# A transformer-like layer on one core: operand builders ordered behind the bank copies, their splits two products behind their loads, and the sums of the FFN down weights made in FFN up

## The chip, the core and the metric

The kernel runs on one core of one Trainium2 chip. The metric is the time of one execution on the device in microseconds (us). Before the change three executions took 1679.03, 1671.73 and 1673.55 us, median 1673.55. The core has a matrix engine (TensorE, PE in the profile, with its weight loads as PEld), two elementwise engines that matter here (VectorE = DVE, ScalarE = ACT), GpSimd (POOL) and the sync engine (SP), which issues nearly all DMAs. The program lists the instructions of each engine in one order, and the trace shows each elementwise engine and SP go through its list in that order; engines wait for each other through semaphores.

## The reference, cut to what matters

One layer over 1024 positions of width 1024, all in float32:

- `h = RMSNorm(x)`, then one wide product `h @ w_in` (1024 to 7168 columns) whose parts feed a retention branch (4 heads, chunked recurrence, group norm, swish gate) and a gated linear recurrence (causal convolution, block-diagonal gates, a scan over positions, GeLU gate).
- Each branch has an output product (`w_ret_o`, `w_lru_o`, 1024 x 1024), the two are merged by sigmoid gates, and `x = x + mix @ w_out`.
- `h = RMSNorm(x)`; `gate, val = split(h @ ffn_w_up)` (1024 to 2 x 3072); a causal convolution of width 3 and GeLU on `gate`; `x = x + (gelu(gate) * val) @ ffn_w_down` (3072 to 1024). A last RMSNorm gives the output.

## The kernel before, in words

**How a product is made exact enough.** Every float32 operand tile of 128 x 512 is split into two reduced-precision float32 tiles: `split` (L165) casts on ScalarE (`hi`, L168) and subtracts on VectorE (`lo`, L169). One product then takes three matmul passes (`PASSES`, L111): hi*hi, hi*lo, lo*hi. An operand tile costs one ScalarE and one VectorE instruction and holds two tile buffers.

**Jobs.** A job computes 256 x 1024 outputs from a 256 x 1024 block of weights (the stationary side, `A11..A22`) and an operand kept on chip (`op`, keys `B11, B12, B21, B22` with j = 0..3, each a split pair). A standard job (`mm_std`, L317; matmuls on L331) takes 8 products of 12 matmuls. A fast job (`mm_fast`, L378; matmuls on L388) is a Strassen-like scheme with 7 products of 12 matmuls; it needs the sums `T1 = B12 - B11`, `T2 = B22 - T1`, `T3 = B12 - B22`, `T4 = B21 - T2` of the operand, split too. In the fast job the bank X is used in a chain: after a product `keep` (L400) copies X on ScalarE (L403), and only then may the next product of X accumulate onto it. `total` (L412) adds a bank to a copy on VectorE (L414), `more` (L406) adds an earlier result read from DRAM (L409). The order of the products is A11 B11, S1 T1, S2 T2, A12 B21, S3 T3, A22 T4, S4 B22, and the first product of the next job is put ahead of the last of the present one.

**Two streams beside the products.** At the end of each product the program calls `build(BRATE)` (L286) and `advance(RATE)` (L304). `build` steps generators in `builders`, which make the operand of a later stage: `operand` (L984) loads 16 blocks and splits them, up to 3 loads ahead of the one it splits (`reads`, L532), then `tsets` (L540) loads the same 16 blocks again, makes the four sums for one j after another (subtractions on L545, L548, L551, L553) and splits them. A step has a cost, and a call of `build` spends up to 3.0: five splits at 0.6. It stops while fewer than 20 of the 81 buffers (`NU`, 128 x 512 float32 each) are free (`RESERVE`). `need` (L296) forces the builder when a product asks for a key that isn't there. `advance` steps the generators in `back`, the work that follows a job (recurrence, retention, and the like), by one unit.

**What sets the order.** The instructions are traced in program order with priorities (`NOW` 3000 for the bank copies and adds, `SOON` 400 for the builders), and a scheduler then lists them engine by engine, once, before the run. It takes the instruction of highest priority among those which its own model of times holds ready. So an instruction of a builder may be listed ahead of a bank copy which is traced earlier, when the model has its data there first. On the chip the engine then waits in that order.

**Where builders work.** `og` (operand of the four standard ret_o jobs, from DRAM tensor `og_d`) is built during the last job of the input product; `u` (from `u_d`, for lru_o: one standard and three fast jobs) during the last ret_o job and the standard lru_o job; `h2` (for FFN up, from tiles on chip) at the start of FFN up; and `dop[0..2]`, the FFN down weights `w_dn` in three groups g, each used by one standard and three fast jobs (t = 0..3). `dop[0]` is built from the last FFN up job on, `dop[g+1]` from job t = 3 of group g on. FFN down adds up its three groups in DRAM (`x1_d`): from_x1 (L1262) reads, L1276 writes. FFN up is 24 jobs, whose `post_ff` (L1208) writes `ff_d`, which FFN down reads as its stationary side.

In the profile's names buffer numbers and digits are left out: `u` is one of the 81 buffers, `w` one of 22 weight buffers, `g` and `a` are PSUM banks, `x_d` is `x1_d` and `t_d` is `t1_d`.

Of the kernel before, what the change touches and what calls it, by code (L numbers as in the profile page):

```python
# [11 lines left out]
F32 = mybir.dt.float32  # L12
# [5 lines left out]
P = 128  # L18
D = 1024
T = 1024  # L20
KT = 8
TH = 512
# [64 lines left out]
class Units:  # L87
# [11 lines left out]
    def get(self, dt=F32):  # L99
        i = self.q.popleft()  # L100
        self.count += 1
        t = self.pool.tile(self.shape, dt, tag=f"{self.name}{i}", name=f"{self.name}{i}_{self.count}")
        self.at[id(t)] = (i, t)
        return t
# [3 lines left out]
            self.q.append(self.at.pop(id(t))[0])  # L108


PASSES = ((0, 0), (0, 1), (1, 0))  # L111
NU = 81
NW = 22
# [3 lines left out]
RATE = 1.0  # L117
BRATE = 3.0
RESERVE = 20
NOW, SOON, OLD = 3000, 400, 800  # L120
FAST_RO = 0
RO_T = 9
# [7 lines left out]
def tile_trunk_layer(ctx, tc, x, xt, positions, params, consts, normf, w_in, w_ro, w_lo,  # L130
# [23 lines left out]
    sg_d = pdr.tile([2, KT, P, T], F32, tag="sg", name="sg_d")  # L154
    t1_d = pdr.tile([KT, P, T], F32, tag="t1", name="t1_d")
    x1_d = pdr.tile([T, D], F32, tag="x1", name="x1_d")
    ff_d = pdr.tile([3, 8, 2, P, 4, P], F32, tag="ff", name="ff_d")

    def pc(name, i):
# [2 lines left out]
    def hp(offset=1500):  # L162
        return tc.high_priority(offset=offset)

    def split(src, get=get):  # L165

        hi, lo = get(F32R), get(F32R)
        S.copy(hi, src)  # L168
        V.tensor_sub(lo, src, hi.bitcast(F32))  # L169
        return hi, lo  # L170

    def drop(s):
        put(*s)
# [4 lines left out]
    class Job:  # L178
        def __init__(self, src, op, emit, post=None, fast=False, last=False, drop12=False,
                     pre=None, fetch=None, order=None):  # L180
            self.pre = pre
            self.order = order or (("A11", "A21", "A22", "A12") if fast else ORD_T)
            self.fetch, self.got = fetch, {}
            self.src, self.op, self.emit, self.post = src, op, emit, post
            self.fast, self.last, self.drop12 = fast, last, drop12
            self.raw, self.blk = {}, {}
# [8 lines left out]
            return self.got.pop((m, h))  # L195

    queue = []
    state = {"load": None, "prep": None, "blocks": 0, "raws": 0, "hp": False}

    def loads():  # L200
        i = 0
# [83 lines left out]

    def build(budget, reserve=RESERVE):  # L286

        with hp(SOON):
            while builders and budget > 0 and len(U) >= reserve:
                c = next(builders[0], None)  # L290
                if c is None:
                    builders.popleft()
                else:
                    budget -= c

    def need(op, key):  # L296
        with hp(SOON):
            while key not in op:
                if next(builders[0], None) is None:
                    builders.popleft()  # L300
        return op[key]


# [74 lines left out]
    def mm_fast(jb, op):  # L378
        X, Y, Z = psg.get(), psg.get(), psg.get()

        def prod(bank, an, bn, first):
            pump((jb, an))
            w = jb.blk[an]
            n = 0
            for j in range(4):
                c = slice(128 * j, 128 * j + 128)
                for a, b in PASSES:
                    PE.matmul(bank, w[a][:, c], need(op, (bn, j))[b], start=first and n == 0, stop=n == 11,  # L388
                              skip_group_check=True)
                    n += 1  # L390
            W.put(*w)
            state["blocks"] -= 1
            if jb.last:
                for j in range(4):
                    drop(op.pop((bn, j)))
            pump()
            build(BRATE)
            advance(RATE)

        def keep(bank):  # L400
            u = get()
            with hp(NOW):
                S.copy(u, bank)  # L403
            return u

        def more(u, m, c):  # L406
            if jb.pre is not None and (m, c) in jb.pre:
                acc = jb.take(m, c)
                V.tensor_add(u, u, acc)  # L409
                put(acc)  # L410

        def total(u, bank, m, c):  # L412
            with hp(NOW):
                V.tensor_add(u, bank, u)  # L414
            jb.emit(m, c, u, u)

        prod(X, "A11", "B11", True)
        s1 = keep(X)
        yield
        jb.ask(0, 0)  # L420
        prod(Z, "S1", "T1", True)
        prod(X, "S2", "T2", False)
        u2 = keep(X)
        more(s1, 0, 0)
        jb.ask(1, 1)
        prod(Y, "A12", "B21", True)
        total(s1, Y, 0, 0)
        psg.put(Y)
        jb.ask(1, 0)
        prod(X, "S3", "T3", False)  # L430
        u3 = keep(X)
        more(u3, 1, 1)
        total(u3, Z, 1, 1)
        yield
        jb.ask(0, 1)
        prod(X, "A22", "T4", False)
        jb.emit(1, 0, X, None)
        psg.put(X)
        more(u2, 0, 1)
        prod(Z, "S4", "B22", False)  # L440
        total(u2, Z, 0, 1)
        psg.put(Z)

# [88 lines left out]
    def reads(fetch, keys, ahead):  # L532

        keys, got = deque(keys), deque()
        while keys or got:
            while keys and len(got) <= ahead:
                got.append(fetch(*keys.popleft()))
            yield got.popleft()

    def tsets(op, fetch, ahead=2):  # L540
        tiles = reads(fetch, [(n, j) for j in range(4) for n in ("B11", "B12", "B21", "B22")], ahead)
        for j in range(4):
            b11, b12, b21, b22 = (next(tiles) for _ in range(4))
            t1, t2 = get(), get()
            V.tensor_sub(t1, b12, b11)  # L545
            op["T1", j] = split(t1)
            yield 1.2
            V.tensor_sub(t2, b22, t1)  # L548
            op["T2", j] = split(t2)
            yield 1.2  # L550
            V.tensor_sub(b12, b12, b22)  # L551
            op["T3", j] = split(b12)
            V.tensor_sub(t2, b21, t2)  # L553
            op["T4", j] = split(t2)
            put(t1, t2, b11, b12, b21, b22)
            yield 2.4

# [426 lines left out]
    def operand(op, fetch, sums=True):  # L984

        keys = [(n, j) for n in ("B11", "B21", "B12", "B22") for j in range(4)]
        for key, t in zip(keys, reads(fetch, keys, 3)):
            op[key] = split(t)
            put(t)
            yield 0.6  # L990
        if sums:
            yield from tsets(op, fetch)
# [234 lines left out]
    def down_op(g):  # L1227
        def fetch(n, j):
            t = get()
            kh, c = int(n[1]) - 1, int(n[2]) - 1  # L1230
            SY.dma_start(t, w_dn[8 * g + 4 * kh + j, :, TH * c:TH * c + TH])
            return t

        yield from operand(dop[g], fetch)

    builders.append(tsets(h2, lambda n, j: keep2[n, j]))
    NF = FF // P
    dop = [{} for _ in range(3)]

    def up_post(i):  # L1240
        def fn():
            if i == NF - 2:
                builders.append(down_op(0))
            with hp(OLD) if i >= NF - 3 else nullcontext():
                post_ff(i)
        return fn

    run([Job(pair_src(w_up, i), h2, emit_to(gv), up_post(i), fast=i >= STD_U, last=i == NF - 1,
# [132 lines left out]
```

## Time and profile before

| | |
|---|---|
| runs shown | 1679.03, 1671.73, 1673.55 us; median 1673.55 us |
| the profiled execution's own time | 1681.74 us |
| its span, first to last instruction | 1680.0 us |
| mean granted TensorE clock | 0.994 |
| busy: PE, DVE, ACT | 1629.2, 1288.6, 885.0 us |

The profiled execution is 8.2 us above the median of the others, and 1.7 us of its time lie outside the span. A busy time is the union of an engine's instructions. Consecutive matmuls overlap (one shows about 392 ns, one starts every 0.227 us), so a PE busy time without gaps doesn't by itself mean that it runs at full pace: the granted clock and the number of matmuls in a stretch have to be read with it. In a row of waits or of the timeline, `<-` stands before what ended the idle time.

By the lines of the matmuls, the input product and its branches take the span up to about 640 us, ret_o and lru_o up to about 840, w_out and the second norm up to about 980, FFN up to about 1405, and FFN down the rest.

### The profile page before, as it was taken

What the parts mean: (1) busy time and instruction counts of PE and PEld (TensorE: products, weight loads), DVE (VectorE), ACT (ScalarE), POOL (GpSimd) and SP (SyncE); (2) the same over time, 40 slices, a digit from 0 to 9 for tenths busy, and PEclk for the clock granted to TensorE, in tenths of its full rate; (3) what the DMA queues carried; (4) which work ended last, traced back from release to release, by engine and by line L of the source; (5) the groups of instructions that cost most, each with busy time, mean ns of one, the idle gap of its engine ahead of it and who ended that gap; (6) DMA issues with size and microseconds to landing.
All of it is one profiled execution on the core that took longest, in us unless ns stands there. A gap on an engine that the chain in (4) does not pass through costs nothing.

```text
span 1680.0 us, 21179 instructions
## 1 busy us (share of the span) xinstructions
PE 1629.2 (97%) x7224; PEld 1332.5 (79%) x7224; DVE 1288.6 (77%) x2366; ACT 885.0 (53%) x1480; POOL 40.6 (2%) x60
## 2 busy tenths in 40 slices
PE   8999999999999999998989999999999999999997
PEld 6888788888888877886768778888888887777776
DVE  8998768666888889857871797677776778878786
ACT  7654443535678877753430464444444455443554
POOL 0001000000000000000000000000000000000000
PEclk9999999999999999999999999999999999999999
DMA  8243212131333348656463122222222247687751
GB/s 292 86 157 96 84 55 88 51 94 45 113 114 107 125 138 266 208 162 235 132 201 105 53 82 88 82 88 82 82 84 85 84 128 235 226 256 245 249 203 76
DMA packets 120524, 225.97 MB, mean 135 GB/s; under 512 B 14048, under 2 KB 14176, under 8 KB 120416
## 3 DMA queue, kind: packets, MB, share of 16 engines
q1 hardware_dynamic: 116192, 210.99, 39.4%
q0 software_dynamic: 4224, 13.64, 2.1%
q8 instruction: 56, 0.92, 0.2%
q14 instruction: 52, 0.43, 0.1%
HBM read 164.80 MB, written 54.53 MB: 131 GB/s over the span
## 4 chain that ended last, share of the span: by engine, by line
PE 50%; DVE 9%; DMA 7%; ACT 2%; issue 2%; SPq 0%; DVEq 0%; ACTq 0%
PE g L388 38%; PE g L331 5%; PE g L1183 4%; DVE u L169 2%; PE a L815 2%; DMA u<-w_dn 2%; DVE w L169 1%; DMA u<-u_d 1%; DMA x_d<-u 1%; DMA t_d<-u 1%; DMA u<-x_d 1%; DVE u L414 0%; PE a L514 0%; ACT u L168 0%; DVE u L798 0%
## 5 line engine op out<-in xcount | busy, mean ns | idle before, releaser
L388 PE MATMUL g<-u,w 128*128 128x512 f32 x5124 | 1208.7, 394 | 25.3 <-ACT u L403 18.1
L388 PEld LDWEIGHTS g<-u,w 128*128 128x128 f32 x5124 | 959.8, 189 | 232.6 <-ACT u L403 25.1
L168 ACT CAST w<-w 128x512 fp32r<-128x512 f32 x471 | 291.0, 620 | 371.0 <-PE g L388 290.8
L169 DVE TENSOR_TENSOR w<-w,w 128x512 fp32r<-128x512 f32 x471 | 322.3, 685 | 91.7 <-ACT w L168 86.9
L331 PE MATMUL g<-u,w 128*128 128x512 f32 x960 | 226.1, 392 | 3.1 <-ACT u L168 2.8
L168 ACT CAST u<-u 128x512 fp32r<-128x512 f32 x232 | 139.5, 620 | 155.9 <-DVE u L553 21.0
L331 PEld LDWEIGHTS g<-u,w 128*128 128x128 f32 x960 | 180.5, 189 | 41.9 <-ACT u L168 3.3
L169 DVE TENSOR_TENSOR u<-u,u 128x512 fp32r<-128x512 f32 x232 | 155.0, 686 | 40.6 <-ACT u L168 28.4
L414 DVE TENSOR_TENSOR u<-g,u 128x512 f32<-128x512 f32 x183 | 125.6, 686 | 60.5 <-PE g L388 47.1
L403 ACT COPY u<-g 128x512 f32<-128x512 f32 x183 | 106.2, 580 | 73.4 <-PE g L388 73.3
L1183 PE MATMUL g<-u,u 128*128 128x512 f32 x384 | 90.1, 392 | 2.1 <-DVE u L169 2.0
L1183 PEld LDWEIGHTS g<-u,u 128*128 128x128 f32 x384 | 71.3, 188 | 17.9 <-DVE u L169 3.1
L1216 DVE SCALAR_TENSOR_TENSOR u<-u,par,u 128x511 f32<-128x511 f32 x96 | 71.7, 747 | 6.2 <-ACT u L1213 5.4
L1221 POOL DMA_DIRECT2D ff_d<-u x48 | 36.1, 752 | 1256.0 <-DVE u L1220 1256.0
L247 DVE TENSOR_TENSOR w<-w,w 128x512 f32<-128x512 f32 x61 | 42.0, 689 | 21.8 <-DMA w<-w_up 11.4
L815 PE MATMUL a<-u,u 128*128 128x512 f32 x192 | 48.7, 393 | 2.3 <-ACT u L168 1.6
L1185 DVE TENSOR_TENSOR u<-g,u 128x512 f32<-128x512 f32 x16 | 11.0, 691 | 49.2 <-PE g L1183 49.2
L1213 ACT ACTIVATE u<-u,par 128x512 f32<-128x512 f32 x48 | 39.2, 817 | 15.1 <-DVE u L414 14.9
L815 PEld LDWEIGHTS a<-u,u 128*128 128x128 f32 x192 | 35.4, 188 | 11.9 <-ACT u L168 3.0
L250 DVE TENSOR_TENSOR w<-w,w 128x512 f32<-128x512 f32 x61 | 41.9, 688 | 0.9
L263 DVE TENSOR_TENSOR w<-w,w 128x512 f32<-128x512 f32 x61 | 41.8, 686 | 0.4
L256 DVE TENSOR_TENSOR w<-w,w 128x512 f32<-128x512 f32 x61 | 41.8, 685 | 0.3
(173 smaller groups left out, 1150.0 us busy)
## 6 DMA issues: line engine op xcount, KB each, us to landing
w<-w_in SPq DMA_DIRECT2D x112, 256.0 KB, 2.7
w<-w_up SPq DMA_DIRECT2D x96, 256.0 KB, 2.6
u<-w_dn SPq DMA_DIRECT2D x96, 256.0 KB, 4.3
u<-x_d SPq DMA_DIRECT2D x56, 256.0 KB, 4.5
x_d<-u SPq DMA_DIRECT2D x48, 256.0 KB, 3.2
ff_d<-u POOLq DMA_DIRECT2D x48, 256.0 KB, 2.5
w<-ff_d SPq DMA_DIRECT2D x48, 256.0 KB, 3.6
u<-x SPq DMA_DIRECT2D x32, 256.0 KB, 5.3
```

The source lines that it names most:

```text
L168: S.copy(hi, src)
L169: V.tensor_sub(lo, src, hi.bitcast(F32))
L247: V.tensor_add(s1, a21, a22)
L250: V.tensor_sub(s1, s1, a11)
L256: V.tensor_sub(a11, a21, a11)
L331: PE.matmul(ps[h], w[a][:, c], o[b], start=n == 0, stop=n == 23)
L388: PE.matmul(bank, w[a][:, c], need(op, (bn, j))[b], start=first and n == 0, stop=n == 11, skip_group_check=True)
L403: S.copy(u, bank)
L414: V.tensor_add(u, bank, u)
L815: PE.matmul(ps, wg[g][a][:, cs], xs[k][b], start=q == 0, stop=q == 5)
L1183: PE.matmul(ps, o[a][:, 128 * t:128 * t + 128], wo[k][b], start=n == 0, stop=n == 23)
L1216: V.scalar_tensor_tensor(c[:, s:], src[:, :TH - s], w, c[:, s:], ALU.mult, ALU.add)
```

## The change

It has four parts.

1. *Order.* A class `Behind` wraps ScalarE and VectorE for the builders (`BS`, `BV`): each instruction which a builder issues through them gets a dependency, without a semaphore, on the last bank copy (`keep`) or bank add (`total`) traced before it. The scheduler may not list it ahead of that instruction.
2. *Distance.* `state["tick"]` counts calls of `build`, one for each product. `landed` makes a builder yield 0 until `LAG` = 2 calls have gone by since the load of what it wants to split; `build` ends its call on a 0. `need` switches this off while it forces a builder. The builder of h2, whose tiles are on chip, is left out of it (`here=True`).
3. *Reads ahead.* `operand` reads 7 loads ahead instead of 3, `tsets` 4 instead of 2.
4. *Sums of the down weights.* `down_op` no longer runs `tsets`. After every second FFN up job, `down_sums(g, j)` loads the four blocks of one (g, j) again, makes the four sums on VectorE and stores them to a new DRAM tensor `td_d`; it is a generator in `back`, one step for each product. `down_op` then loads the 16 finished sums from `td_d`, in the order T1, T2, T3, T4, and splits them. The number of loads per group stays 32.

```diff
+class Behind:
+    def __init__(self, tc, eng):
+        self.tc, self.eng, self.last = tc, eng, None
+        self.how = mybir.DependencyInfo(mybir.DependencyClass.NoSync, mybir.DependencyReason.DATA)
+    def __getattr__(self, name):
+        fn = getattr(self.eng, name)
+        def call(*args, **kw):
+            ins = fn(*args, **kw)
+            if self.last is not None:
+                self.tc.add_manual_dep(ins.ins, self.last, self.how, reason="behind the banks' copies")
+            return ins
+        return call
...
+LAG, AHEAD_B, AHEAD_T = 2, 7, 4
...
+    td_d = pdr.tile([3, 4, 4, P, TH], F32, tag="td", name="td_d")
...
-    def split(src, get=get):
+    def split(src, get=get, S=S, V=V):
...
+    BS, BV = Behind(tc, S), Behind(tc, V)
...
                 if c is None:
                     builders.popleft()
+                elif c == 0:
+                    break
                 else:
                     budget -= c
+        state["tick"] += 1
...
     def need(op, key):
         with hp(SOON):
+            state["force"] = True
             while key not in op:
                 if next(builders[0], None) is None:
                     builders.popleft()
+            state["force"] = False
...
-                S.copy(u, bank)
+                BS.last = S.copy(u, bank).ins.name
...
-                V.tensor_add(u, bank, u)
+                BV.last = V.tensor_add(u, bank, u).ins.name
...
-                got.append(fetch(*keys.popleft()))
+                got.append((state["tick"], fetch(*keys.popleft())))
...
+    def landed(tick):
+        while state["tick"] - tick < LAG and not state["force"]:
+            yield 0
...
-    def tsets(op, fetch, ahead=2):
+    def tsets(op, fetch, ahead=AHEAD_T, here=False):
...
-            b11, b12, b21, b22 = (next(tiles) for _ in range(4))
+            four = [next(tiles) for _ in range(4)]
+            if not here:
+                yield from landed(four[-1][0])
+            b11, b12, b21, b22 = (t for _, t in four)
...
-        for key, t in zip(keys, reads(fetch, keys, 3)):
-            op[key] = split(t)
+        for key, (tick, t) in zip(keys, reads(fetch, keys, AHEAD_B)):
+            yield from landed(tick)
+            op[key] = split(t, get, BS, BV)
...
-        yield from operand(dop[g], fetch)
+        yield from operand(dop[g], fetch, False)
+        def sums(n, j):
+            t = get()
+            SY.dma_start(t, td_d[g, int(n[1]) - 1, j])
+            return t
+        keys = [(f"T{i}", j) for i in (1, 2, 3, 4) for j in range(4)]
+        for key, (tick, t) in zip(keys, reads(sums, keys, AHEAD_B)):
+            yield from landed(tick)
+            dop[g][key] = split(t, get, BS, BV)
+            put(t)
+            yield 0.6
+
+    def down_sums(g, j):
+        b = {}
+        for kh in range(2):
+            for c in range(2):
+                b[kh, c] = get()
+                SY.dma_start(b[kh, c], w_dn[8 * g + 4 * kh + j, :, TH * c:TH * c + TH])
+        yield 1.0
+        t = get()
+        V.tensor_sub(t, b[0, 1], b[0, 0])
+        ST.dma_start(td_d[g, 0, j], t)
+        put(b[0, 0])
+        yield 1.0
+        V.tensor_sub(b[0, 1], b[0, 1], b[1, 1])
+        ST.dma_start(td_d[g, 2, j], b[0, 1])
+        put(b[0, 1])
+        yield 1.0
+        V.tensor_sub(b[1, 1], b[1, 1], t)
+        ST.dma_start(td_d[g, 1, j], b[1, 1])
+        put(t)
+        yield 1.0
+        V.tensor_sub(b[1, 0], b[1, 0], b[1, 1])
+        ST.dma_start(td_d[g, 3, j], b[1, 0])
+        put(b[1, 0], b[1, 1])
...
-    builders.append(tsets(h2, lambda n, j: keep2[n, j]))
+    builders.append(tsets(h2, lambda n, j: keep2[n, j], here=True))
...
             with hp(OLD) if i >= NF - 3 else nullcontext():
                 post_ff(i)
+            return down_sums(i // 8, i % 8 // 2) if i % 2 == 0 else None
```

More of the change, by code (lines that the diff above doesn't have):

```diff
@@ L197, in tile_trunk_layer @@
     queue = []
-    state = {"load": None, "prep": None, "blocks": 0, "raws": 0, "hp": False}
+    state = {"load": None, "prep": None, "blocks": 0, "raws": 0, "hp": False, "tick": 0, "force": False}
     def loads():
@@ L536, in reads @@
             while keys and len(got) <= ahead:
-                got.append(fetch(*keys.popleft()))
+                got.append((state["tick"], fetch(*keys.popleft())))
             yield got.popleft()
-    def tsets(op, fetch, ahead=2):
+    def landed(tick):
+        while state["tick"] - tick < LAG and not state["force"]:
+            yield 0
+    def tsets(op, fetch, ahead=AHEAD_T, here=False):
         tiles = reads(fetch, [(n, j) for j in range(4) for n in ("B11", "B12", "B21", "B22")], ahead)
         for j in range(4):
-            b11, b12, b21, b22 = (next(tiles) for _ in range(4))
+            four = [next(tiles) for _ in range(4)]
+            if not here:
+                yield from landed(four[-1][0])
+            b11, b12, b21, b22 = (t for _, t in four)
             t1, t2 = get(), get()
-            V.tensor_sub(t1, b12, b11)
-            op["T1", j] = split(t1)
+            BV.tensor_sub(t1, b12, b11)
+            op["T1", j] = split(t1, get, BS, BV)
             yield 1.2
-            V.tensor_sub(t2, b22, t1)
-            op["T2", j] = split(t2)
+            BV.tensor_sub(t2, b22, t1)
+            op["T2", j] = split(t2, get, BS, BV)
             yield 1.2
[L551 to L554, printed above, removed]
+            BV.tensor_sub(b12, b12, b22)
+            op["T3", j] = split(b12, get, BS, BV)
+            BV.tensor_sub(t2, b21, t2)
+            op["T4", j] = split(t2, get, BS, BV)
             put(t1, t2, b11, b12, b21, b22)
```

## The prediction

> **What bounds the kernel now.** First the page's head and busy times, then the list of TensorE's waits.
>
> ```profile
> span 1680.0 us, 21179 instructions
> PE 1629.2 (97%) x7224; PEld 1332.5 (79%) x7224; DVE 1288.6 (77%) x2366; ACT 885.0 (53%) x1480; POOL 40.6 (2%) x60
> ```
> ```profile
> PE g L388 <- ACT u L403: 18.1, 12, 3.8
> PE g L364 <- ACT u L581: 6.8, 1, 6.8
> PE g L388 <- DVE u L414: 4.0, 3, 1.8
> PE g L388 <- ACT u L168: 3.1, 2, 2.1
> PE g L331 <- ACT u L168: 2.8, 1, 2.8
> ```
>
> The matrix engine sets the end: it is idle for 1680.0 - 1629.2 = 50.8 us. The change doesn't touch its work, so all that it can win is in those gaps and in what they do to the clock. The largest cause is the bank copy of the fast jobs (L403), late twelve times. Next, the busy times by stretch: the builders of og and u, FFN up, and FFN down while builders run.
>
> ```profile
> 630.00:830.00 200.00, 190.87 (x813) 154.76 (x812) 155.80 (x261) 112.63 (x168) 0.00 (x0) 0.97 0.62 203
> 985.00:1385.00 400.00, 400.00 (x1763) 330.35 (x1762) 291.59 (x479) 195.99 (x329) 32.32 (x43) 1.00 0.29 91
> 1385.00:1640.00 255.00, 240.50 (x1040) 194.93 (x1039) 208.31 (x354) 123.81 (x224) 3.76 (x5) 0.99 0.72 233
> ```
>
> The columns after the stretch are its length, then busy time and count of PE, PEld, DVE, ACT, POOL, then clock, DMA share and GB/s. FFN up has no gap at all. The two stretches with builders have 9.1 and 14.5 us, nearly half of all, and the DMA is busy there. How such a gap comes about stands in the timeline (start, duration, what; in brackets the idle time before it). In FFN down:
>
> ```profile
> 1576.33 5.87 SPq L1231 DMA_DIRECT2D u<-w_dn  x7
> 1578.42 0.62 ACT L168 CAST u<-u 128x512 fp32r<-128x512 f32 x1 [1.69 <-DMA u<-w_dn]
> 1578.94 0.58 ACT L403 COPY u<-g 128x512 f32<-128x512 f32 x1
> 1579.57 3.04 PE L388 MATMUL g<-u,w 128*128 128x512 f32 x12 [2.37 <-ACT u L403]
> ```
>
> A builder's cast waits for its load. The bank copy is listed behind it, starts the moment the cast is through, and the matrix engine has stood for 2.37 us. The same on VectorE, and one of another origin:
>
> ```profile
> 1517.18 0.69 DVE L553 TENSOR_TENSOR u<-u,u 128x512 f32<-128x512 f32 x1
> 1517.78 0.69 DVE L414 TENSOR_TENSOR u<-g,u 128x512 f32<-128x512 f32 x1
> 1518.53 3.01 PE L388 MATMUL g<-u,w 128*128 128x512 f32 x12 [1.67 <-DVE u L414]
> ```
> ```profile
> 1458.58 0.69 DVE L247 TENSOR_TENSOR w<-w,w 128x512 f32<-128x512 f32 x1 [2.04 <-DMA w<-ff_d]
> 1461.73 1.35 PE L388 MATMUL g<-u,w 128*128 128x512 f32 x3 [1.82 <-DVE u L414]
> ```
>
> In the first a sum of `tsets` (L553) stands ahead of the bank add. In the second it is a weight load of the jobs themselves, with no builder in it. The gaps before 840 us:
>
> ```profile
> 649.16 7.33 PE L388 MATMUL g<-u,w 128*128 128x512 f32 x24 [2.77 <-ACT u L403]
> ```
> ```profile
> 756.38 5.43 SPq L998 DMA_DIRECT2D u<-u_d  x11
> 771.66 0.49 PE L331 MATMUL g<-u,w 128*128 128x512 f32 x1 [2.84 <-ACT u L168]
> 793.48 6.69 PE L388 MATMUL g<-u,w 128*128 128x512 f32 x22 [2.11 <-ACT u L168]
> ```
>
> The first is again a copy, in the og stage. At 771.66 and 793.48 it is the operand itself that isn't there: the u builder is late, because the recurrence that writes `u_d` ends late and its loads queue.
>
> **What a gap costs beside its length.** In rows of 2 us after the og gap:
>
> ```profile
> 648.00:650.00 2.00, 0.84 (x3) 0.75 (x4) 1.55 (x3) 1.86 (x5) 0.00 (x0) 0.93 0.92 321
> 650.00:652.00 2.00, 2.00 (x6) 1.54 (x6) 2.00 (x5) 1.28 (x2) 0.00 (x0) 0.50 0.53 155
> 652.00:654.00 2.00, 2.00 (x8) 1.59 (x7) 0.61 (x2) 0.43 (x1) 0.00 (x0) 0.71 0.94 343
> ```
> ```profile
> 1494.00:1496.00 2.00, 1.82 (x8) 1.52 (x9) 1.69 (x4) 1.69 (x4) 0.00 (x0) 1.00 1.04 383
> ```
>
> The clock falls to 0.93, 0.50, 0.71 of full, which loses 2 x (0.07 + 0.50 + 0.29) = 1.7 us. After the gap of 1494 us there is no such fall. So a long gap costs 1.7 us more, a short one nothing. The Trainium skill, page "TensorE: Matmul & The Clock Gate", section "HAM oscillation — how this bites in real kernels", gives as its rule that gaps of the matrix engine longer than about 3.4 us bring the clock down. This trace differs: a gap of 2.77 us did. By the rule the og term below would lose its 1.7 us, and the forecast would be 1.7 us later; the trace decides.
>
> **The change, part by part.**
>
> *Order and distance in FFN down.* Of the 14.5 us I leave the 1.82 of the weight load: 12.7 us hang on builders. What ScalarE waited for from 1380 to 1640 us says how they divide:
>
> ```profile
> ACT u L168 <- DMA u<-w_dn: 17.9, 9, 3.9
> ACT u L168 <- DVE u L548: 12.5, 8, 3.5
> ACT u L168 <- DVE u L553: 12.4, 7, 3.7
> ...
> ACT u L168 <- DVE u L545: 7.6, 3, 2.7
> ```
> ```profile
> L545 DVE TENSOR_TENSOR u<-u,u 128x512 f32<-128x512 f32 x12 | 8.0, 684 | 0.0
> ```
>
> Waits for the sums are 12.5 + 12.4 + 7.6 = 32.5 us against 17.9 for loads, 64 to 36. The sums leave this stretch: four lines of 12 at 0.684 us, 33 of VectorE's 208 busy us. So 0.64 x 12.7 = 8.1 us go. For the loads, the distance has to be set against the landing:
>
> ```profile
> 530.57 27.21 PE g L388 x120
> ```
> ```profile
> u<-w_dn SPq DMA_DIRECT2D x96, 256.0 KB, 4.3
> ```
>
> A product of 12 matmuls takes 27.21 / 10 = 2.72 us, two of them 5.44, more than the median landing of 4.3 us. But eight loads are asked for at once, and the SP row at 1576.33 gives 5.87 / 7 = 0.84 us for each: the last is issued after 6.7 us. I take half of this share, 2.3 us, between none and all 4.6. The term is 10.4 us, bounds 0 and 12.7; below nothing is a rival.
>
> The builder must also be in time. Its six `build` calls in the last job of a group go: load, wait, five splits, three, four, four. All 16 B keys are then split as the next standard job begins, and that needs only the first eight at once. The 16 T keys take five of its eight calls. T1 now comes whole before T2, where `tsets` went through three sets of four before the last T1. So there is room, two products or more, and I cost the lateness at nothing. If that room is gone, the price is that of 771.66: 2.84 + 1.7 = 4.5 us at each place.
>
> *The same in og and u.* og has the one gap, 2.77 + 1.7 = 4.5 us; I take 4.0 (bounds 0 and 4.5). In u, 9.1 - 2.77 = 6.4 us are left, of which the 2.84 of 771.66 hang on the recurrence and stay. u keeps its sums, and its `tsets` waits two calls more for its second loads. Of the other 3.5 us I take half, 1.7. The bounds are a loss of 4.5, one more late operand, and a gain of 6.4 with two falls of the clock, 9.8.
>
> *The sums in FFN up.* Twelve calls of `down_sums`, each with four loads, four subtractions and four stores. Their 48 subtractions take 48 x 0.684 = 32.8 us of VectorE, which is idle there for 400 - 291.6 = 108 us. The 96 transfers of 256 KB are 25.2 MB in 400 us, 63 GB/s on top of 91, below the 233 of FFN down. All go through SP's queue: a store stands there until its subtraction is through, and weight loads behind it. A subtraction stands in VectorE's queue until its loads land, and bank adds behind it. The row for such a wait in FFN up (from 985 to 1380 us):
>
> ```profile
> DVE w L247 <- DMA w<-w_up: 11.4, 18, 2.6
> ```
>
> Eighteen waits, the longest 2.6 us, made no gap. I take 1.5 us for all, one gap of the mean size in FFN down (14.5 us in ten). The lower bound is nothing; the upper is a gap in each call, 12 x 1.45 = 17.4 us. Without the idle time of VectorE the 32.8 us would lie bare.
>
> **The sum.** 10.4 + 4.0 + 1.7 - 1.5 = 14.6 us. From the profiled execution's 1681.74 us (1680.0 of span, 1.74 around it) that makes 1667.1; this execution lay 8.2 us above the median of 1673.55. From the median it makes **1659 us**.
>
> **The rivals.**
>
> *The transfers bound the builders.* The waits for loads stay and take in the copies again; only what hung on the sums goes. For it: the DMA share of 0.72, and bursts of eight. Against it: 0.29 to 0.72 leave room, and the copies can no longer be listed behind splits of earlier steps. Then 8.1 us at most come off, less 1.5, and with some of that lost to a longer burst I put it at 1673.55 - 5.5 = 1668.
>
> *All gaps of builders go.* Both stretches lose all but the weight load's: 9.1 + 12.7, and three falls of the clock, 5.1: 26.9 us, 1646.7. For it: each has a builder's instruction in it. Against it: u waits for its data, not for its place.
>
> *Operands late (the other side).* Splits come two products after their loads and behind the bank copies, so each operand is ready later than today. If the first keys are not split when a standard job starts, the matrix engine stands at each of five starts (og, u, three groups) for 2.84 + 1.7 = 4.5 us: 22.7. With 14.6 won elsewhere that is 1681.7; and if the four first T1 products are late too, 18.2 more, 1699.9. It decides where a builder is more than two products behind its steps. For it: the gap of 771.66 is of this kind, VectorE is busy for 208 of 255 us, and the limit of 20 free buffers can stop a builder that holds eight in flight. Against it: 33 us less on VectorE, and T1 first.
>
> *FFN up tears.* The upper bound above: 1659 + 15.9 = 1675.
>
> **How the numbers follow.** The forecast has 0.50, the transfers 0.20, all gaps gone 0.10, operands late 0.14, FFN up 0.06. A measurement of this kernel tells about 0.5%, 8.4 us, from no change: faster is below 1665.2, slower above 1681.9. Faster takes nearly all of the forecast (0.46), all gaps gone (0.10) and a quarter of the transfers (0.05): 0.61. Slower is the late operands with little from elsewhere: 0.14. The rest, 0.25, is no change. The range goes from 1646, just below all gaps gone, to 1681, into the late operands; it leaves out about 0.06 below and 0.13 above. The forecast's own is 1652 to 1666, from its bounds.
>
> **What would show each step.** Right: in FFN down no row of L388 waiting for L403 or L414 over 1 us except behind a weight load, waits of ScalarE for L545 to L553 gone from there, FFN up with PE at 400 of 400 and VectorE near 324, the gap at 649 gone with its fall of the clock. The transfers: casts still waiting for `w_dn` or `td_d`, and L403 behind them. Operands late: gaps named after L168 or L169 on L331 and at the start of T1 products. FFN up: gaps between 985 and 1385. The prediction is wrong if the gaps go and the time stays, or if new ones take their place.

## The result and the profile after

The changed kernel took 1658.44, 1659.14, 1657.22, 1659.84 and 1660.16 us, median **1659.14 us**, against 1671.73 us (1666.51 to 1679.03) for the kernel before beside it. The ratio is **0.9914, 95% interval 0.9895 to 0.9932**. The forecast was 1659 us, the range 1646 to 1681, faster with a chance of 0.61.

The profiled execution of the kernel after has 1658.44 us and a span of 1656.7 us; that of before had 1680.0. So 23.3 us lie between the two profiles, while the medians differ by 12.6: the profiled execution of before was a long one. That is why I had it profiled once more (below). TensorE's idle time in the profiles went from 50.8 to 34.4 us and its busy time from 1629.2 to 1622.3 us.

Line numbers have shifted: L388 is now L417 (fast jobs), L331 is L360 (standard jobs), L403 is L432 (bank copy), L414 is L443 (bank add), L1183 is L1221 (w_out), L998 is L1036 (loads of og_d and u_d). The instructions of `split` and `tsets` that go through `Behind` show as L122 whatever they do; the other splits are L188 and L189. TensorE's waits in the whole execution (after the colon the sum in us, how often, and the longest):

```profile
PE g L417 <- ACT u L432: 13.3, 8, 4.7
PE g L393 <- ACT u L618: 5.8, 1, 5.8
PE a L852 <- ACT u L188: 1.6, 2, 0.9
...
PE g L417 <- DVE u L122: 0.9, 1, 0.9
PE a L852 <- DVE u L189: 0.9, 1, 0.9
PE g L417 <- ACT u L122: 0.6, 1, 0.6
```

The copies are late 13.3 us in 8 places instead of 18.1 in 12, the bank adds no longer at all, and the long wait for an operand by L331 (2.8 us) is gone. But the longest copy gap has grown from 3.8 to 4.7 us. The stretches (the last begins and ends earlier, as FFN down now does):

```profile
630.00:830.00 200.00, 192.78 (x838) 157.44 (x837) 161.83 (x270) 116.19 (x176) 0.00 (x0) 0.99 0.65 210
985.00:1385.00 400.00, 399.02 (x1760) 330.03 (x1759) 309.25 (x512) 190.14 (x318) 32.30 (x43) 1.00 0.46 150
...
1375.00:1620.00 245.00, 240.98 (x1050) 197.15 (x1049) 190.69 (x337) 124.54 (x234) 3.76 (x5) 0.99 0.74 245
```

FFN down has 4.0 us of gaps where there were 14.5. FFN up carries 150 GB/s instead of 91 and its VectorE 309 us instead of 292, and loses 1.0 us. All of FFN down's remaining gaps over 0.3 us in the timeline, but for the last bank copy at the very end:

```profile
1396.48 3.06 PE L417 MATMUL g<-u,w 128*128 128x512 f32 x12 [1.11 <-ACT u L432]
1402.70 7.36 PE L417 MATMUL g<-u,w 128*128 128x512 f32 x24 [1.81 <-ACT u L432]
1595.60 46.53 PE L417 MATMUL g<-u,w 128*128 128x512 f32 x204 [0.97 <-ACT u L432]
```

The og gap stands at the same place as before, and is longer:

```profile
648.13 0.62 ACT L122 CAST u<-u 128x512 fp32r<-128x512 f32 x1 [3.32 <-DMA y_d<-u]
648.66 0.58 ACT L432 COPY u<-g 128x512 f32<-128x512 f32 x1
649.29 4.61 PE L417 MATMUL g<-u,w 128*128 128x512 f32 x12 [4.75 <-ACT u L432]
```

The cast waits here not for its load but for a store, `y_d<-u`: the buffer it is to write is still being read out.

And the late operand of u. Before, the queue of SP and what it waited for:

```profile
755.79 0.68 DVE L853 TENSOR_TENSOR u<-u,u 128x512 f32<-128x512 f32 x1
756.38 5.43 SPq L998 DMA_DIRECT2D u<-u_d  x11
...
762.72 0.32 SPq L854 DMA_DIRECT2D u_d<-u  x1
...
768.06 0.32 SPq L998 DMA_DIRECT2D u<-u_d  x1
```

After:

```profile
753.20 0.68 DVE L890 TENSOR_TENSOR u<-u,u 128x512 f32<-128x512 f32 x1
753.91 0.38 SPq L891 DMA_DIRECT2D u_d<-u  x1
754.38 5.45 SPq L1036 DMA_DIRECT2D u<-u_d  x8
```

The last row of `u_d` was ready at 756.5 us before, but its store was listed behind eleven loads and left 6.2 us later. Only at 768.06 could the load of that row follow. After, the store leaves as soon as the row is ready. So the wait that I had put down to the recurrence was one for a place in SP's queue. Of the 32 loads of `u_d`, 28 are issued before that store, so at least twelve of them are second reads.

### The profile page after: what moved, and what is told of

Its sections match the earlier page's. It is cut to its first block, busy times and chain, and to the rows that moved or that the text cites. A ratio compares the mean times of both kernels' runs of the same rounds, so it can differ in the third digit from the quotient of the medians.

```text
span 1656.7 us, 21338 instructions
## 1 busy us (share of the span) xinstructions
PE 1622.3 (98%) x7224; PEld 1329.8 (80%) x7224; DVE 1287.0 (78%) x2366; ACT 880.2 (53%) x1480; POOL 40.6 (2%) x60
## 5 line engine op out<-in xcount | busy, mean ns | idle before, releaser
L417 PE MATMUL g<-u,w 128*128 128x512 f32 x5124 | 1204.0, 393 | 14.9 <-ACT u L432 13.3
L417 PEld LDWEIGHTS g<-u,w 128*128 128x128 f32 x5124 | 958.2, 188 | 218.7 <-ACT u L432 18.6
L188 ACT CAST w<-w 128x512 fp32r<-128x512 f32 x471 | 291.3, 620 | 413.2 <-PE g L417 286.9
L189 DVE TENSOR_TENSOR w<-w,w 128x512 fp32r<-128x512 f32 x471 | 321.9, 684 | 83.4 <-ACT w L188 73.7
L360 PE MATMUL g<-u,w 128*128 128x512 f32 x960 | 223.5, 390 | 0.0
L360 PEld LDWEIGHTS g<-u,w 128*128 128x128 f32 x960 | 179.3, 188 | 38.0 <-ACT u L686 0.3
L443 DVE TENSOR_TENSOR u<-g,u 128x512 f32<-128x512 f32 x183 | 125.3, 685 | 50.5 <-PE g L417 40.4
L432 ACT COPY u<-g 128x512 f32<-128x512 f32 x183 | 106.1, 580 | 65.0 <-PE g L417 62.8
L122 DVE TENSOR_TENSOR u<-u,u 128x512 fp32r<-128x512 f32 (+1 forms) x192 | 122.0, 683 | 15.1 <-ACT u L122 10.4
L122 ACT CAST u<-u 128x512 fp32r<-128x512 f32 x160 | 90.4, 619 | 45.0 <-DVE u L122 15.3
L1221 PE MATMUL g<-u,u 128*128 128x512 f32 x384 | 90.0, 392 | 1.0 <-ACT u L188 0.9
L1221 PEld LDWEIGHTS g<-u,u 128*128 128x128 f32 x384 | 71.3, 188 | 16.6 <-ACT u L188 1.4
L271 DVE TENSOR_TENSOR w<-w,w 128x512 f32<-128x512 f32 x61 | 42.0, 689 | 25.3 <-DMA w<-ff_d 9.6
L188 ACT CAST u<-u 128x512 fp32r<-128x512 f32 x72 | 43.3, 619 | 26.5 <-DMA u<-w_out 11.2
L189 DVE TENSOR_TENSOR u<-u,u 128x512 fp32r<-128x512 f32 x72 | 47.9, 683 | 4.0 <-ACT u L188 3.7
L274 DVE TENSOR_TENSOR w<-w,w 128x512 f32<-128x512 f32 x61 | 41.9, 687 | 1.0
```

Source lines behind the costliest of these rows:

```text
L122: ins = fn(*args, **kw)
L271: V.tensor_add(s1, a21, a22)
L274: V.tensor_sub(s1, s1, a11)
L360: PE.matmul(ps[h], w[a][:, c], o[b], start=n == 0, stop=n == 23)
L432: BS.last = S.copy(u, bank).ins.name
L443: BV.last = V.tensor_add(u, bank, u).ins.name
```

## The experiments

Ratios are of each kernel to the kernel before, run on the same chip beside it; no_s, no_d, lag_only and ahead_only ran on another chip than the others below. The three parts that can be had apart are the **order** (`Behind`), the **distance** (`LAG` with the reads 7 and 4 ahead) and the **sums** in FFN up. Gaps are the sums of the timeline's gaps of PE in one profiled execution, in us: "og" around 650 us, "u" up to w_out's neighbourhood at 832, "w_out" from there to 905, "up" from 970 to 1375, "down" from 1375 us on but for the last 0.68. "Falls" counts how often the granted clock goes below 0.9 in rows of 2 us between 640 us and the last bank copies of FFN down.

| kernel | parts | ratio, 95% interval | og | u | w_out | up | down | falls |
|---|---|---|---|---|---|---|---|---|
| before | none | 1 | 2.9 | 6.1 | 6.0 | 0 | 14.5 | 5 |
| before_again | none | (one execution) | 3.2 | 5.4 | 5.5 | 0 | 11.3 | 4 |
| o_only | order | 0.9989, 0.9972 to 1.0006 | 3.2 | 4.0 | 2.7 | 0 | 11.1 | 7 |
| d_only | distance | 0.9929, 0.9909 to 0.9949 | 3.1 | 1.0 | 3.1 | 0 | 4.9 | 2 |
| s_only | sums | 1.0048, 1.0030 to 1.0067 | 3.2 | 6.5 | 3.6 | 2.4 | 10.2 | 7 |
| no_s | order, distance | 0.9976, 0.9962 to 0.9990 | 5.0 | 3.0 | 3.6 | 0 | 9.7 | 3 |
| no_o | distance, sums | 0.9974, 0.9959 to 0.9989 | 3.7 | 1.1 | 3.2 | 2.1 | 6.9 | 5 |
| no_d | order, sums | 0.9985, 0.9971 to 1.0000 | 3.0 | 3.6 | 2.2 | 1.3 | 10.5 | 3 |
| after | all three | 0.9914, 0.9895 to 0.9932 | 4.8 | 2.5 | 3.0 | 1.0 | 3.9 | 2 |

A fall costs about 1.7 us, as the prediction worked out from its rows. Take the gaps of the table and 1.7 us for each fall off the spans of the profiled executions, which go from 1655.4 to 1680.0 us: what is left is 1638 to 1642 us in all nine. So the gaps and the falls together account for most of what sets these kernels apart.

**The order alone.** Of the change only `Behind` and its two uses in `keep` and `total`:

```diff
-LAG, AHEAD_B, AHEAD_T = 2, 7, 4
+LAG, AHEAD_B, AHEAD_T = 0, 3, 2
...
-        yield from operand(dop[g], fetch, False)
+        yield from operand(dop[g], fetch)
+        return
...
-            return down_sums(i // 8, i % 8 // 2) if i % 2 == 0 else None
+            return None
```

> Only the order (builders behind bank copies and adds); loads 3 and 2 ahead as before, no distance, the down sums in FFN down as before. Theory A (the prediction: most of the loss in FFN down hangs on the sums' work, a smaller part on the place of the splits): the ten gaps of FFN down shrink from 14.5 us to about 10, the u stage keeps its late operands (about 6 us), time 0.3% below before, ratio 0.997. Rival B (the place of the splits ahead of the bank copies is the whole cause): gaps in FFN down under 4 us, ratio 0.992. Rival C (a gain between the last ret_o job and w_out that comes from any other order): about 11 us gone there, FFN down as before, ratio 0.994.

Measured 1668.64 us, ratio 0.9989 (0.9972 to 1.0006): no change that can be told. The casts in FFN down wait for `w_dn` 5.5 us instead of 17.9, yet 11.1 us of gaps are left, near theory A's 10. Rival B's gaps of under 4 us didn't come, but the edit doesn't test it to the end: the order holds a builder's cast behind the copies traced before it, not behind the next one. At 1433.91 us such a cast has waited 3.25 us for VectorE, the copy follows at 1435.68, and TensorE has stood 1.83 us.

**Distance and reads ahead alone.**

```diff
-    BS, BV = Behind(tc, S), Behind(tc, V)
+    BS, BV = S, V
```

and the sums back in FFN down as in the edit before.

> Only the distance of two products and the reads 7 and 4 ahead; order and down sums as before. Theory A: the waits of casts for w_dn (17.9 us on ScalarE) fall by more than half, the waits for sums (32.5 us) stay, gaps in FFN down about 11 us, ratio 0.998. Rival D (the distance is what counts): gaps in FFN down under 5 us and the operand gaps of u gone, ratio 0.992. Rival E (more loads in flight only recycle buffers sooner): the gap before the last job of the input product grows from 2.8 to 4.7 us, as in the changed kernel, ratio 1.001.

Measured 1658.57 us, ratio **0.9929** (0.9909 to 0.9949): an interval that overlaps with that of the whole change. FFN down has 4.9 us of gaps, with all its sums still in it. What ScalarE waited for there (1385 to 1640 us) decides about my split of the gaps; first this kernel, then, for the kernel with the sums alone, the same view:

```profile
ACT u L188 <- DVE u L590: 13.9, 9, 2.4
ACT u L188 <- DVE u L582: 12.7, 7, 4.2
...
ACT u L188 <- DVE u L588: 6.2, 5, 1.9
...
ACT u L188 <- DVE u L585: 4.8, 8, 0.7
...
ACT u L188 <- DMA u<-w_dn: 1.2, 2, 0.7
```
```profile
ACT u L188 <- DMA u<-w_dn: 23.3, 9, 9.4
ACT u L188 <- DMA x_d<-u: 10.3, 4, 3.7
ACT u L188 <- DMA u<-td_d: 6.0, 5, 1.7
```

With the distance the waits for sums (L582, L585, L588, L590: the four subtractions of `tsets`) are 37.6 us, no less than the 34.3 of before (the prediction's 32.5 and the 1.8 for L551, T3), and of the 14.5 us of gaps 4.9 are left, 3.0 of them at bank adds. The waits for `w_dn` fell from 17.9 to 1.2. So the sums needn't leave FFN down for the gaps to go, and the size of ScalarE's waits doesn't tell what they cost TensorE. That doesn't mean that sums were never in the way. In the kernel before, six copies of FFN down are late, and three of them stand directly behind a cast that waited for a sum. One of the three:

```profile
1443.94 0.62 ACT L168 CAST u<-u 128x512 fp32r<-128x512 f32 x1 [1.91 <-DVE u L548]
1444.46 0.58 ACT L403 COPY u<-g 128x512 f32<-128x512 f32 x1
1445.09 1.20 PE L388 MATMUL g<-u,w 128*128 128x512 f32 x4 [1.11 <-ACT u L403]
```

The other two are the gaps of 1.47 and 1.44 us at 1499.57 and 1584.96, each behind a cast that waited 2.72 us for L545: 4.0 us in all, and 4.5 us at the same three places of before_again. The three behind a wait for a load of `w_dn` are the gaps of 1.60, 1.51 and 2.37 us, 5.5 in all. In u the store of the last row leaves at 753.36 us, when its product is through, as in the kernel after; with the order alone it still stands behind eleven loads until 759.82. Theory A (mine) falls, rival D holds.

**The sums alone.** `BS, BV = S, V` as above, with `LAG, AHEAD_B, AHEAD_T = 0, 3, 2`; the sums made in FFN up and read back.

> Only the down weights' sums made in FFN up and read back; order, distance and reads ahead as before. Theory A: 8.1 of the 12.7 us in FFN down go, FFN up keeps its 400 busy of 400 us, ratio 0.996. Rival F (loads, not sums, hold the splits): FFN down keeps over 10 us of gaps, ratio 1.000. Rival G (FFN up tears): gaps between 985 and 1385 us of over 5 us, ratio above 1.001.

Measured 1680.09 us, ratio **1.0048** (1.0030 to 1.0067): slower. FFN down keeps 10.2 us of gaps, where casts wait more for loads than before, 23.3 + 6.0 us. Rival F's gaps came, its ratio of 1.000 didn't. The sum of all gaps is about that of before_again, 25.9 against 25.4 us; what is added are falls of the clock, seven against four, after the gaps of 3.06 and 2.75 us in FFN down among others. FFN up has a part in it: gaps of 0.4 and 1.95 us at its start, and a fall (0.63, 0.51) after the second, some 4 us. That is less than rival G's 5 us of gaps, but it isn't nothing.

**All but the order.** The changed kernel with `BS, BV = S, V`.

> The changed kernel without the order: distance, reads ahead and sums kept. Theory A: gaps in FFN down rise from 4.0 to about 6 us, ratio to before 0.993. Rival B (the place is the whole cause): gaps in FFN down back above 9 us, ratio 0.997. Rival C (the u stage's gain belongs to the order): the 11 us between 734 us and the first product of w_out come back, ratio 0.998.

Measured 1666.51 us, ratio 0.9974 (0.9959 to 0.9989): the interval lies above that of the whole change. The gaps in FFN down are near theory A's 6 us, the ratio is that of rival B. The clock makes most of the difference to the changed kernel: five falls where that one has two, among them one after each gap in FFN down and one after a gap of 2.08 us at the start of FFN up. The u stage keeps its gain, 1.1 us of gaps, so rival C falls. In FFN down there are three gaps, all behind bank copies: 3.26, 1.77 and 1.84 us. The second of them:

```profile
1484.42 0.62 ACT L188 CAST u<-u 128x512 fp32r<-128x512 f32 x1 [2.06 <-DMA u<-td_d]
1484.95 0.61 ACT L188 CAST w<-w 128x512 fp32r<-128x512 f32 x1
1485.47 0.58 ACT L432 COPY u<-g 128x512 f32<-128x512 f32 x1
...
1486.10 1.20 PE L417 MATMUL g<-u,w 128*128 128x512 f32 x4 [1.77 <-ACT u L432]
```

It is the pattern of before, with `td_d` in place of `w_dn`. The gap of 3.26 us isn't of that kind: its casts had waited 2.39 us for a store to `ff_d`.

**All but the sums.** The changed kernel with the sums back in FFN down.

> The changed kernel with the sums back in FFN down (order, distance and reads ahead kept). Theory H: nothing is lost, ratio 0.992 to 0.993, gaps in FFN down about 5 us, ScalarE's waits for sums back at about 32 us without gaps of PE. Rival A (the prediction: the sums' work is most of the loss): gaps in FFN down up to about 11 us, ratio 0.997.

Measured 1667.98 us, ratio 0.9976 (0.9962 to 0.9990), above that of the distance alone. The order, added to the distance, costs something when the sums are in FFN down. The gaps there are of another kind:

```profile
1440.90 1.16 ACT L122 CAST u<-u 128x512 fp32r<-128x512 f32 x2 [1.50 <-DVE u L122]
1441.33 0.68 DVE L1349 TENSOR_TENSOR u<-g,u 128x512 f32<-128x512 f32 x1
1441.57 1.23 PE L417 MATMUL g<-u,w 128*128 128x512 f32 x3 [3.11 <-ACT u L122]
```

TensorE waits for the split operand itself, as VectorE still works at sums and splits. Such gaps (named after L122) are 0.77, 3.11, 1.69, 1.00 and 0.29, 6.9 of the 9.7 us. This is "operands late", the rival that I had put on the other side. Expecting the ratio to stay was wrong for theory H, and theory A fits the number 0.997 but not for its reason.

**All but distance and reads ahead.** The changed kernel with `LAG, AHEAD_B, AHEAD_T = 0, 3, 2`.

> The changed kernel without distance and reads ahead (order and sums kept). Theory H: the gain goes with it; sums alone had cost 0.5% and order alone won 0.1%, so ratio 1.002, casts waiting for w_dn and td_d over 12 us in FFN down. Rival L (the order takes away what the sums alone cost): ratio 0.996.

Measured 1670.08 us, ratio 0.9985 (0.9971 to 1.0000). Casts wait 10.7 us for `td_d` and 4.1 for `w_dn` in FFN down, 10.5 us of gaps. Theory H's waits of over 12 us came, its ratio of 1.002 didn't. The gain goes with the distance; but the order takes away what the sums alone cost (1.0048 against 0.9985, intervals apart), as rival L said, if not by as much.

**The two halves of the distance.** No order, sums in FFN down, and either only the distance (`LAG, AHEAD_B, AHEAD_T = 2, 3, 2`) or only the reads ahead (`0, 7, 4`).

> Only the distance of two products, with reads 3 and 2 ahead as before (four loads in flight); order and sums as before. Theory H (a load must have been on its way long enough before its split is listed): the waits of casts for w_dn go from 17.9 us to under 4, gaps in FFN down under 6 us, ratio 0.993 like distance and reads ahead together. Rival I (with four in flight a builder passes four keys in two products, so it comes late): PE waits for operands at the starts of the standard jobs, ratio 1.003 or more. Rival J (neither half works alone): ratio 0.998.

> Only the reads 7 and 4 ahead, no distance; order and sums as before. Theory H: reads ahead put loads earlier too, but the first splits of each builder still follow their loads at once; casts wait for w_dn about 10 us, gaps in FFN down about 9 us, ratio 0.997. Rival K (reads ahead are the whole): gaps in FFN down under 6 us, ratio 0.993. Rival E (buffers recycled sooner): more waits for x_d stores, ratio 1.000 or more.

Measured 1674.91 us, ratio 1.0014 (1.0000 to 1.0029), and 1671.00 us, ratio 0.9984 (0.9970 to 0.9998). The gaps in FFN down are 15.6 and 9.0 us, in u 3.0 and 3.6. Neither half has the gain of both (0.9929). For the reads ahead theory H's figures came: waits for `w_dn` of 9.0 us (10 expected) and gaps of 9.0. For the distance alone theory H fails, and with it the account that late loads are the whole matter: the waits for `w_dn` went down to 5.2 us, near the 4 that it expected, and the gaps didn't go. The two longest are 4.31 and 2.69 us, both at bank copies. The last wait of the casts ahead of the first is 1.58 us for a store to `ff_d`, and ahead of the second 4.40 us for a store to `x1_d`, not for a load. Rival I is the nearest in ratio (1.003), but it had said that operands would come late at the starts of the standard jobs, and that isn't where the time went. Rival J's 0.998 lies outside the interval.

**The kernel before, once more.**

> The kernel before, profiled once more, to see which gaps belong to it and which to that one execution (1681.74 us, over its median). If a gap is the program's, it stands again within 0.5 us: og 2.8, u 2.8 and 2.1, FFN down 13 to 15 us in all. The 3.8 us gap just ahead of w_out is the one I expect to be smaller, about 1.5 to 2 us, since the kernel with only the sums moved, which changes nothing there, showed 1.5; span 1665 to 1672 us.

Its span was 1672.9 us, just above what I expected, its time 1674.72. The gaps that stand again: og 3.16 (2.77), u 2.11 and 2.11 (2.84 and 2.11), FFN down ten, 11.3 us in all, below the 13 to 15 that I expected. The one ahead of w_out was 1.90 us instead of 3.75, as expected. So single gaps move by up to 2 us from one execution to the next, and the first profile had several of the large ones: FFN down's gain is 7.4 us against this profile and 10.6 against the first.

**The order only where it seemed to pay.** `operand` gets the engines as arguments, `BS, BV` for the down weights and plain `S, V` for og and u; `tsets` uses `BS, BV` for h2 alone:

```diff
-    def operand(op, fetch, sums=True):
+    def operand(op, fetch, sums=True, S_=S, V_=V):
...
-            op[key] = split(t, get, BS, BV)
+            op[key] = split(t, get, S_, V_)
...
-        yield from operand(dop[g], fetch, False)
+        yield from operand(dop[g], fetch, False, BS, BV)
```

> The changed kernel with the order for the down and h2 builders only; og and u free of it. Theory H2 (distance cures the loads; the order is needed only where td_d loads come behind the bank copies, and elsewhere makes operands late): u falls from 2.5 to about 1.0 us of gaps, og from 4.8 to about 3.1 to 3.7, FFN down stays at about 4, ratio 0.989 to 0.990. Rival M (each listing falls out anew, no part has a price of its own): gaps anywhere, ratio between 0.992 and 0.998.

Measured 1656.53 us, ratio 0.9908 (0.9890 to 0.9925). u falls to 1.4 us and FFN down stays low, 3.2; og keeps 4.7. Not to be told from the changed kernel, but the gaps did what was expected in two of three places. Rival M (each listing falls out anew) doesn't fit this.

**Fewer buffers in flight for og.**

```diff
-    def operand(op, fetch, sums=True):
+    def operand(op, fetch, sums=True, ahead=AHEAD_B):
...
-        for key, (tick, t) in zip(keys, reads(fetch, keys, AHEAD_B)):
+        for key, (tick, t) in zip(keys, reads(fetch, keys, ahead)):
...
-        builders.append(operand(og, from_dram(og_d), False))
+        builders.append(operand(og, from_dram(og_d), False, 3))
```

> The changed kernel with og's builder reading 3 ahead instead of 7. Theory (eight buffers in flight make the ring short, so a split's destination is a buffer whose y_d store is still on its way): the gap at 649 us falls from 4.8 to about 3 us, ratio 0.990 to 0.991. Rival (the stretch is bound by its transfers, 280 GB/s, whoever reads): the gap stays between 2.6 and 5 us with another load or store named, ratio as before this edit, 0.991 to 0.993.

Measured 1655.22 us, ratio 0.9906 (0.9887 to 0.9924). In place of one gap of 4.75 us there are two, 1.40 and 0.83:

```profile
646.66 0.58 ACT L432 COPY u<-g 128x512 f32<-128x512 f32 x1 [0.78 <-DMA y_d<-u]
...
647.30 3.01 PE L417 MATMUL g<-u,w 128*128 128x512 f32 x12 [0.83 <-ACT u L432]
```

The stage's gaps fall from 4.8 to 2.4 us, below the 3 that were expected, and the clock no longer falls after them; it is the one kernel without a fall up to the last copies. A wait for the `y_d` store is still there, 0.78 us, at the copy's own buffer. That agrees with a ring of buffers made short by the loads in flight. The reads ahead aren't enough for the long wait, though: casts wait 3.0 to 3.3 us for the `y_d` store in the three kernels that have them and the order in og (after, no_s, order_wout), but 0.74 us in no_o and 0.55 in order_down, which have no order there. It is the lowest median of all, but its interval overlaps with that of the changed kernel, so a gain over it isn't shown.

**The order for w_out's splits too.**

```diff
-                wo[k] = split(r)
+                wo[k] = split(r, get, BS, BV)
```

> The changed kernel with the order also for the splits of w_out, which the change leaves ahead of the last bank copies of lru_o. Theory (a cast waiting for its load ahead of a bank copy is what makes a gap): the 2.0 us gap just ahead of w_out goes, w_out's own start waits at most 1 us more, ratio 0.990. Rival (the splits come too late then): the first product of w_out waits 2 us or more, ratio 0.992 or above.

Measured 1660.26 us, ratio 0.9935 (0.9916 to 0.9954). The gap just ahead of w_out went from 2.02 to 0.68 us, and w_out's own first products waited 1.66 instead of 0.95. 0.6 us net in that place; the ratio shows no gain and is the rival's (0.992 or above), though the wait of 2 us that the rival named didn't come. The gap goes as the theory said; in the time nothing of it is seen.

## Why the prediction was right, and where it was not

*The time and the sum.* 1659.0 forecast, 1659.14 measured. That they meet so closely is luck. The forecast took 14.6 us off a median of 1673.55; measured were 12.6, off 1671.73. And the terms were not those of the sum: og had the wrong sign, u and w_out were too small, and of five falls of the clock before and two after the sum had only the one in og, which stayed. Of the signs named for being right, one came in full, that ScalarE no longer waits for sums in FFN down; copies late by 1.11 and 1.81 us are left there, and the gap at 649 us has grown.

*FFN down: 10.4 us.* 10.6 us of gaps went against the profile that the sum used, 7.4 against the second. The size is near; the division into 8.1 for the sums and 2.3 for the loads failed. The step that failed is "The sums leave this stretch", "So 0.64 x 12.7 = 8.1 us go". It shared the gaps out by what ScalarE waited for and took away the share of the sums. But a wait of ScalarE only costs if a bank copy stands behind it while TensorE needs that bank: of the 34.3 us of waits for sums, 7.4 stood directly ahead of a late copy, and they made 4.0 us of gaps. And what is listed ahead of a copy changes with the kernel. With the sums alone gone, casts waiting for loads stood ahead of copies and 10.2 us of gaps were left; with the distance alone, the sums stayed and 4.9 were left. The list had also left out 9.1 us of waits for stores to `x1_d`. "I take half of this share, 2.3 us" was too low as far as the loads go: `w_dn` waits went from 17.9 to 1.2 us with distance and reads ahead. Why these two are needed together stays open: low waits for `w_dn` don't do it by themselves (5.5 us with the order alone and 5.2 with the distance of two products alone, where 11.1 and 15.6 us of gaps were left).

*What the parts do together.* I summed them; they don't add. The sums win nothing without the order (1.0048 alone, 0.9974 with the distance) and the order wins nothing without the sums (0.9989, and 0.9976 with the distance, where the distance alone has 0.9929). Together they do no harm: 0.9914. The rows say what they run into when added singly: without the order, casts for `td_d` are listed ahead of copies; with the order but with the sums in place, the operands come late. Why the sums alone raise the waits for loads is only argued: before, a split of T waited for a chain of subtractions, in which its loads had time to land; now it is a load and a cast.

*og: 4.0 us.* Wrong in sign: its gaps grew from 2.9 to 4.8 us. The step "I take 4.0 (bounds 0 and 4.5)" had no bound below nothing. It took the wait for a load away and didn't ask what the eight buffers in flight do to the 81, or what the order then holds up: the cast waited 3.32 us for a store that was still reading the buffer it was to write. With reads 3 ahead the longest gap fell to 1.4 us, and without the order the long wait for the store isn't there either (no_o, order_down).

*u: 1.7 us.* Too small: 6.1 us of gaps (5.4 in the second profile) became 2.5. The step that failed is "2.84 of 771.66 hang on the recurrence and stay". The recurrence was through at 756.5 us; the store stood behind eleven loads in SP's queue. I had quoted the very row, 5.43 us for x11, and read it as the loads' own lateness. The profiles divide cleanly by it. In the five profiles without distance or reads ahead (before twice, o_only, s_only, no_d) the store leaves 5.5 to 6.6 us after its row is ready, and the standard job waits 1.3 to 2.8 us for an operand at about 770 us. In all the others it leaves within 1.5 us and that gap isn't there. Either half is enough for this: the distance alone has 1.5 us, the reads ahead alone 0.3. But each alone has a gap of 3.0 or 3.6 us later in the stage, so this queue isn't the whole of u.

*w_out: nothing.* Gaps from 6.0 to 3.0 us, but 5.5 in the second profile of before and 3.6 in the kernel with only the sums moved, so part of it is that execution. Not forecast, and the cause isn't settled.

*FFN up: 1.5 us.* Measured 1.0 between 985 and 1385 us; PE has 380.00 of 380 from 1000 to 1380. VectorE is at 309 us, not 324: it has 512 instructions there instead of 479, 47 of them the new subtractions, so 14 others now lie outside the stretch. The size of the term is near, its place another one. All seven kernels with the sums moved have a gap of 1.0 to 2.1 us at the start of FFN up, and none of the seven profiles without has one; in six of them a bank copy waits there for a store to `ff_d`, which GpSimd issues (1.92 us in the kernel after). The prediction had looked for the wait behind a subtraction or in SP's queue. After 1.95 and 2.08 us (s_only, no_o) the clock fell too. The rival of twelve gaps falls.

*The clock.* The rule of the Trainium skill, page "TensorE: Matmul & The Clock Gate", section "HAM oscillation — how this bites in real kernels", of gaps over about 3.4 us, is contradicted here again: after 3.08 us in d_only the clock falls to 0.51, after 2.77 before to 0.50. With no gap above 1.4 us in that stage (og_reads3), it stays at 1.00. The prediction's own "a long gap costs 1.7 us more, a short one nothing" doesn't hold by length either: in the kernel before, the clock falls to 0.53 after 1.82 us at 1461.73 and stays at 1.00 after 2.37 us at 1579.57; in the kernel after it falls to 0.50 after 1.81 us at 1402.70. What decides between them no run here shows.

*The rivals.* "Transfers bound the builders" falls: FFN down has a DMA share of 0.74 and 4.0 us of gaps. "All gaps go" didn't come. "Operands late" didn't come for the change as a whole, but stood in the kernel without the sums, with the price of one gap right (3.11 against 2.84 us). I had put it at an operand's first use in a standard job, and it stood at sums in fast ones.

## What to carry to other kernels

An elementwise engine's wait costs only when what is listed behind it is due: read the gap of the busiest engine backwards to the instruction ahead, and don't divide its loss by the waits of the engine that feeds it. What stands ahead today need not be what goes: when the sums left, loads stood in their place. Ask of each store in a queue which loads are listed ahead of it, and what waits for it; a load that nobody needs yet can hold the row that everyone needs. Where a change has parts that meet in one queue, price them together or try them apart: here one part alone had the gain, and each of the other two took some of it back when added singly, and nothing when added together.

## What the runs showed that I had not expected

The same program's single gaps differ by up to 2 us between executions (3.75 and 1.90 us for the one ahead of w_out), and its time by 12.5 us (1666.51 to 1679.03), about as much as the change won; the changed kernel's own five times lie within 2.9 us. After many gaps from 1.8 us on, though not after all, the clock stood at half for about two microseconds and was back within six, which makes such a gap cost about 1.7 us more than it shows. Moving the sums alone left the sum of gaps as it was and still lost 0.5%, as the clock fell more often. That a kernel with fewer long gaps also varies less is consistent with it, but wasn't tried by itself.
